# Low parts of the weights of the second layer's first FFN: VectorE subtraction or accumulating DMA

## The chip, the cores and the metric

The kernel runs on one core of one Trainium2 chip. What is measured is the device time of one execution in microseconds (us). One core has a TensorE (PE, matrix products; PEld is its weight load), a VectorE (DVE), a ScalarE (ACT), a GpSimd (POOL), a SyncE (SP) that issues the loads, and 16 DMA engines that all queues share.

## What is computed

Two small transformers stand one behind the other, on 256 positions of width 1024. The first has two layers, with modulation vectors made from a condition, and carries 256 context positions beside the 256 main ones, so that most of its products have 512 columns. Each layer is an FFN, a token mixer and a second FFN:

```
def _swiglu(h, w1, w3, w2):
    return (jax.nn.silu(h @ w1) * (h @ w3)) @ w2

for l in range(DEPTH):
    ml = _modulation(c, w_ada[l], b_ada[l])
    mc = _modulation(c_ctx[None], w_ada[l], b_ada[l])
    ffn1 = (ffn1_w1[l], ffn1_w3[l], ffn1_w2[l])
    lat = lat + 0.5 * ml[2] * _swiglu(_modulate(lat, norm_ffn1_g[l], ml[0], ml[1]), *ffn1)
    cx = cx + 0.5 * mc[2] * _swiglu(_modulate(cx, norm_ffn1_g[l], mc[0], mc[1]), *ffn1)
    ...
```

w1 and w3 are 1024 x 2816, w2 is 2816 x 1024, all float32. The second transformer (a retention and window layer, an axial attention layer, two MLPs) follows, and is not touched here.

## The kernel before, in words

The products with weights run on TensorE with operands in the type float32r. Each weight and each activation is held as a pair: hi, the value written as float32r, and lo, the value minus hi. mm3 makes three matmuls of each product: hi by hi (L294), hi weight by lo activation (L295), lo weight by hi activation (L296).

The weights lie in HBM in the order in which they are used, cut by plan() into 544 chunks of 128 x 1024 (w2's later thirds: 128 x 896). The class Weights brings them in. For each chunk, SP issues a load into one of 4 raw buffers (dma_to, L135), ACT copies raw into one of 6 hi buffers (hi_to, L145), and DVE writes raw minus hi into one of 5 lo buffers (lo_to, L156). A raw buffer is free again when DVE has read it, a hi or lo buffer when TensorE has done the last matmul on it.

Every engine works through its own queue in order, and the order is that in which the code emits the instructions. In the steady part (step) one chunk is one step: first its 24 matmuls, then the closing work of an earlier step (flush), then ahead_hi, then one tick of a background job, then ahead_lo. In the step of chunk b, ahead_hi goes up to chunk b+5 and ahead_lo up to b+4, as far as there are buffers; SP then loads up to 4 chunks beyond the last lo.

The second layer's first FFN is ffn(1, 0): 68 chunks, in three thirds of w1/w3 pairs (gated, L521 to L526: silu on ACT, product on DVE, hi copy on ACT, lo on DVE) followed by eight w2 chunks each. Its background job is ada: 32 tiles of 512 KB (L264) and a 1 MB condition tile (condb, L269; its silu on ACT is L272), and two DVE reductions a tile (L279), one tile a step.

The first four chunks are used before the steps begin, in tail, which closes the FFN before. I call these chunks F0 to F3, the next F4 and so on; w6 and w7 are the last two chunks of the FFN before. tail does the halves of w6 and w7 for the main positions, calls W.lo_to(W.n_take + 2), which prepares chunks up to F2, does the halves for the context positions, takes the row sums (stats, L369, L373) and broadcasts them (bcast, L383), and makes the new h (make_h: DVE L402, ACT L410, DVE L411). Then F0 to F2 run on the first half. F3 is taken only there, by a call of its own, and its pair is made at that point. Then the second half's h is made, F0 to F2 run on it, W.ahead() prepares F4 to F6, and F3's second half closes the turn.

Of the kernel before, what the change touches and what calls it, by code (L numbers as in the profile page):

```python
# [7 lines left out]
F32 = mybir.dt.float32  # L8
F32R = mybir.dt.float32r
U8 = mybir.dt.uint8  # L10
AF = mybir.ActivationFunctionType
ALU = mybir.AluOpType
# [14 lines left out]
def plan():  # L27

    out = []

    def ffn(l, nm):
        for t0, n in THIRDS:
            for j in range(t0, t0 + n):
                out.append((nm + "_w1", l, 0, 8, j * 128, 128))
                out.append((nm + "_w3", l, 0, 8, j * 128, 128))
            for o in range(8):
                out.append((nm + "_w2", l, t0 * 128, n, o * 128, 128))

    U, V, Q, FW, BW, I, OG = (i * 512 for i in range(7))
    for l in range(2):  # L40
        ffn(l, "ffn1")

        def cols(c0, n):
            for j in range(n):
                out.append(("w_in", l, 0, 8, c0 + j * 128, 128))

        def pairs(name, ly, c0, n):
            for j in range(n):
                out.append((name, ly, 0, 4, c0 + j * 256, 256))
                out.append((name, ly, 512, 4, c0 + j * 256, 256))  # L50

        cols(FW, 2), cols(BW, 2), cols(Q, 2)
        pairs("w_in", l, I, 2)
        cols(FW + 256, 2), cols(BW + 256, 2), cols(Q + 256, 2)
        pairs("w_in", l, V, 2)
        cols(OG + 256, 2), cols(OG, 2), cols(U, 4)
        for o in range(8):
            out.append(("w_out", l, 0, 8, o * 128, 128))
        ffn(l, "ffn2")

    def pairs2(name, c0, n):
        for j in range(n):
            out.append((name, 0, 0, 4, c0 + j * 256, 256))
            out.append((name, 0, 512, 4, c0 + j * 256, 256))

    def mlp(l):
        for j in range(32):
            out.append(("w_mlp_up_2", l, 0, 8, j * 128, 128))
        for o in range(8):
            for q in range(4):  # L70
                out.append(("w_mlp_down_2", l, q * 1024, 8, o * 128, 128))

    for c0, n in ((2048, 4), (4096, 1), (4352, 1), (3072, 4), (0, 2), (512, 2), (1024, 4)):
        pairs2("w_in_even_2", c0, n)
    for r0 in (1024, 0):
        for o in range(8):
            out.append(("w_out_even_2", 0, r0, 8, o * 128, 128))
    mlp(0)
    for c0, n in ((1024, 1), (0, 2), (1280, 1), (512, 2)):
        pairs2("w_in_odd_2", c0, n)  # L80
    for r0 in (0, 512):
        for o in range(4):
            out.append(("w_out_odd_2", 0, r0, 4, o * 256, 256))
    mlp(1)
    return out
# [22 lines left out]
class Pair:  # L108


    def __init__(self, hi, lo=None):
        self.t = [hi, lo]
# [5 lines left out]
class Weights:  # L118


    def __init__(self, nc, flat, rawp, hlp, sizes, nraw, nhl):
        self.nc, self.flat, self.rawp, self.hlp = nc, flat, rawp, hlp
        self.sizes, self.nraw, self.nhl = sizes, nraw, nhl
        self.offs = np.concatenate([[0], np.cumsum(np.array(sizes) * 128)]).tolist()
        self.n = len(sizes)
        self.n_dma = self.n_hi = self.n_lo = self.n_take = 0
        self.raw, self.hl = {}, {}
# [11 lines left out]
    def hi_to(self, i):  # L139
        while self.n_hi <= min(i, self.n - 1):  # L140
            j = self.n_hi
            self.dma_to(j)
            c = self.sizes[j]
            t = self.hlp.tile([128, 1024], F32R, tag="hi", name="hi", bufs=self.nhl)
            self.nc.scalar.activation(out=t[:, :c], in_=self.raw[j][:, :c], func=AF.Copy)  # L145
            self.hl[j] = Pair(t)
            self.n_hi += 1

    def lo_to(self, i):
        while self.n_lo <= min(i, self.n - 1):  # L150
            j = self.n_lo
            self.hi_to(j)
            c = self.sizes[j]
            t = self.hlp.tile([128, 1024], F32R, tag="lo", name="lo", bufs=self.nhl - 1)
            w = self.hl[j]
            self.nc.vector.tensor_tensor(  # L156
                out=t[:, :c], in0=self.raw.pop(j)[:, :c], in1=w[:, 0, :c].bitcast(F32), op=ALU.subtract)
            w.t[1] = t
            self.n_lo += 1
        self.dma_to(self.n_lo - 1 + self.nraw)  # L160
# [10 lines left out]
        self.ahead_lo(rate)  # L171

    def ahead_hi(self, rate=3):
        self.hi_to(min(self.n_hi + rate - 1, self.base + self.nhl - 1))

    def ahead_lo(self, rate=3):
        self.lo_to(min(self.n_lo + rate - 1, self.base + self.nhl - 2))
# [2 lines left out]
def build(tc, T):  # L180
    nc = tc.nc
    vo, nvec = vec_plan()
    sizes = [p[3] * p[5] for p in plan()]
    PS = bass.MemoryType.PSUM
    with ExitStack() as ctx, tc.manual_schedule():
        pool = lambda name, bufs, **k: ctx.enter_context(tc.tile_pool(name=name, bufs=bufs, **k))
# [2 lines left out]
        rawp = pool("rawp", 4)  # L189
        hlp = pool("hlp", 1)  # L190
# [3 lines left out]
        b1 = ctx.enter_context(ExitStack())  # L194
        hp = b1.enter_context(tc.tile_pool(name="hp", bufs=1))

        W = Weights(nc, T["wflat"], rawp, hlp, sizes, 4, 6)

        def tmp(n=512, dt=F32):
            return tp.tile([128, n], dt, tag="t", name="t")  # L200
# [1 line left out]
        def mm_ps():  # L202
            return psm.tile([128, 512], F32, tag="mm", name="mm")
# [94 lines left out]
        def mmA(ps, w, X, nk, t0, t1, k0=0, k1=None, first=True):  # L298

            k1 = nk if k1 is None else k1  # L300
            for k in range(k0, k1):
                mm3(ps[:, t0:t1], w[:, 0, k * 128:(k + 1) * 128], w[:, 1, k * 128:(k + 1) * 128],
                    X[k][:, 0, t0:t1], X[k][:, 1, t0:t1], k == 0, k == nk - 1)
# [3 lines left out]
        def flush():  # L307
            while epis:
                epis.pop(0)()
# [4 lines left out]
        def step(fn, epi=None, rate=3, parts=1):  # L314

            for i, f in enumerate(fn if isinstance(fn, list) else [fn]):
                f()
                if i == 0:
                    flush()
                    W.ahead_hi(rate)  # L320
                    if not lo_last[0]:
                        W.ahead_lo(rate)
                pace[0] += 1
# [3 lines left out]
                if i == 0 and lo_last[0]:  # L327
                    W.ahead_lo(rate)
            if epi is not None:
# [94 lines left out]
        def group_start():  # L424
            ws = W.take(4)
            return ws, [mm_ps() for _ in range(4)]
# [6 lines left out]
        def norm_group(l, i, halves, more=()):  # L433
# [4 lines left out]
            for half, dg in zip(halves, dgs):  # L438
# [3 lines left out]
                for c in range(4):  # L442
                    mmA(ps[c], ws[c], h, 8, half[0], half[1], 4, 8)
                    W.base = W.n_take - 4 + c
                    W.ahead(1)
            return ps
# [538 lines left out]
        with ExitStack() as ph:  # L985
# [106 lines left out]
            for i in range(2):  # L1092
                t = tmp()
# [156 lines left out]
        class Attn:  # L1250


            def __init__(self, kT, vv, bias, sink, perm, scale, pool):
                self.kT, self.vv, self.bias, self.sink, self.perm, self.scale, self.pool = (
                    kT, vv, bias, sink, perm, scale, pool)
                self.heads, self.done = [], 0
# [164 lines left out]
        with ExitStack() as ph:  # L1421
# [99 lines left out]
            for j in range(4):  # L1521
                proj(lambda p, b, j=j: nc.scalar.activation(
                    out=sg[:, b, j * 256:(j + 1) * 256], in_=p[:, :256], func=AF.Silu, scale=rr[:, b:b + 1]),
# [99 lines left out]
            for o in range(8):  # L1623
                (w,) = W.take(1)
                p = mm_ps()
# [6 lines left out]
            for o in range(8):  # L1632
                (w,) = W.take(1)
                p = mm_ps()
# [35 lines left out]
        with ExitStack() as ph:  # L1670
# [34 lines left out]
            for j in range(4):  # L1705
                proj(lambda p, b, j=j: epi_q(p, b, j))
                if j == 1:
                    proj(lambda p, b: nc.scalar.activation(
                        out=vb[:, b, :], in_=p[:, :256], func=AF.Copy, scale=rr[:, b:b + 1]))
# [34 lines left out]
            for half in range(2):  # L1744
# [14 lines left out]
                for o2 in range(2, 4):  # L1759
                    (w,) = W.take(1)  # L1760
                    for i in range(2):
                        o = 2 * o2 + i
                        p = mm_ps()
# [132 lines left out]
```

## Time and profile before

| | us |
|---|---|
| median of 3 runs | 2420.7 (2420.54 to 2421.33) |
| the profiled execution | 2421.72 |
| its span, first to last instruction | 2419.9 |
| PE busy | 2392.5 (99%) |
| DVE busy | 1565.7 (65%) |
| ACT busy | 1013.0 (42%) |
| POOL busy | 58.5 (2%) |
| DMA engines, mean busy share | 45% |

The rows below name a line of the kernel (L156 is line 156), the engine, and output <- inputs. Busy times of different engines lie beside each other. A view by windows shows what each engine did in a stretch; a view of waits shows who had to stand still and for whom; a timeline shows single instructions with their start and length. PE's lengths overlap, since matmuls are pipelined: the distance of two starts is what one costs.

### The profile page before, as it was taken

To read this page: it belongs to the slowest core of one execution; us is meant where nothing else is said; L and a number is where in the kernel's file an instruction comes from. 1 tells how busy PE (TensorE), PEld (TensorE's weight loads), DVE (VectorE), ACT (ScalarE), POOL (GpSimd) and SP (SyncE) were. 2 spreads that over 40 slices of the span, in tenths; PEclk is the share of its full clock that TensorE was granted. 3 is DMA by queue.
4 is the path that set the end of the run, shared out by engine and by line. 5 is a ranking of instruction groups with operands and counts; after the bars stand their busy time and mean duration, and the time that the engine had idled before them with its cause. 6 is when DMAs were issued, how large, how long until landed. Compare 5 with 4: busy or idle time off the path is not lost.

```text
span 2419.9 us, 37688 instructions
## 1 busy us (share of the span) xinstructions
PE 2392.5 (99%) x15240; PEld 2145.0 (89%) x15240; DVE 1565.7 (65%) x2498; ACT 1013.0 (42%) x1649; POOL 58.5 (2%) x102
## 2 busy tenths in 40 slices
PE   7999999999999999999999999999999999999999
PEld 5888888999888888898888899999999999999999
DVE  6777876736478784468763366765576676557753
ACT  4322223455342222342222353654467556446642
POOL 0000000000000000000000000000002000010000
PEclk9999999999999999999999999999999999999999
DMA  8555552312245453235543232345655365553653
GB/s 311 201 191 175 200 190 70 104 54 70 79 160 198 178 196 112 89 133 198 184 149 102 87 100 84 114 157 187 186 193 169 127 201 185 192 166 114 209 190 125
DMA packets 107791, 370.88 MB, mean 153 GB/s; under 512 B 11864, under 2 KB 18008, under 8 KB 107232
## 3 DMA queue, kind: packets, MB, share of 16 engines
q1 hardware_dynamic: 107616, 368.47, 44.9%
q8 instruction: 120, 1.97, 0.3%
q14 instruction: 55, 0.45, 0.1%
HBM read 367.36 MB, written 1.06 MB: 152 GB/s over the span
## 4 chain that ended last, share of the span: by engine, by line
PE 91%; DVE 3%; issue 3%; ACT 2%; DMA 0%; POOL 0%; POOLq 0%; SPq 0%; DVEq 0%; ACTq 0%
PE mm L295 26%; PE mm L296 26%; PE mm L294 26%; PE mm L655 2%; PE mm L1188 2%; PE mm L1189 2%; PE mm L1187 2%; DVE lo L156 1%; PE mm L850 1%; PE mm L849 1%; PE mm L851 1%; ACT hi L145 0%; PE aux L383 0%; PE mm L1284 0%; PE aux L369 0%
## 5 line engine op out<-in xcount | busy, mean ns | idle before, releaser
L294 PE MATMUL mm<-h,hi 128*128 128x512 f32 (+1 forms) x2460 | 834.6, 339 | 3.0 <-ACT h L410 1.9
L296 PE MATMUL mm<-h,lo 128*128 128x512 f32 (+1 forms) x2460 | 829.8, 337 | 0.4 <-DVE lo L156 0.2
L145 ACT ACTIVATE hi<-raw 128x1024 fp32r<-128x1024 f32 (+1 forms) x544 | 563.5, 1042 | 527.1 <-PE mm L295 312.5
L156 DVE TENSOR_TENSOR lo<-raw,hi 128x1024 fp32r<-128x1024 f32 (+1 forms) x544 | 652.3, 1205 | 141.1 <-issue 55.8
L295 PE MATMUL mm<-l,hi 128*128 128x512 f32 (+1 forms) x2076 | 722.6, 348 | 1.1 <-DVE l L1074 0.2
L294 PEld LDWEIGHTS mm<-h,hi 128*128 128x128 f32 x2460 | 465.0, 189 | 56.7 <-ACT h L410 2.2
L296 PEld LDWEIGHTS mm<-h,lo 128*128 128x128 f32 x2460 | 464.7, 189 | 55.0 <-DVE lo L156 1.2
L295 PEld LDWEIGHTS mm<-l,hi 128*128 128x128 f32 x2076 | 392.5, 189 | 56.1 <-DVE l L411 2.7
L294 PE MATMUL mm<-g,hi 128*128 128x256 f32 (+1 forms) x1258 | 409.3, 325 | 0.0
L295 PE MATMUL mm<-g,hi 128*128 128x256 f32 (+1 forms) x1258 | 408.8, 325 | 0.0
L296 PE MATMUL mm<-g,lo 128*128 128x256 f32 (+1 forms) x1258 | 408.8, 325 | 0.0
L279 DVE CUSTOM_DVE_ANT_0 jk<-ada,condb,vec 128x1024 f32<-128x1024 f32 x256 | 328.1, 1282 | 11.7 <-ACT condb L272 7.2
L295 PEld LDWEIGHTS mm<-g,hi 128*128 128x128 f32 x1258 | 236.8, 188 | 22.2
L294 PEld LDWEIGHTS mm<-g,hi 128*128 128x128 f32 x1258 | 236.9, 188 | 22.1
L296 PEld LDWEIGHTS mm<-g,lo 128*128 128x128 f32 x1258 | 236.8, 188 | 22.0
L525 ACT ACTIVATE g<-t 128x512 fp32r<-128x512 f32 (+1 forms) x88 | 50.9, 578 | 350.8 <-DVE t L523 350.8
L417 DVE SCALAR_TENSOR_TENSOR xT<-mm,mods,xT 128x256 f32<-128x256 f32 x192 | 86.0, 479 | 135.7 <-PE mm L296 135.5
L523 DVE TENSOR_TENSOR t<-t,mm 128x512 f32<-128x512 f32 (+1 forms) x88 | 54.6, 620 | 181.2 <-PE mm L296 179.1
L295 PE MATMUL mm<-h,hi 128*128 128x256 f32 x512 | 143.9, 281 | 0.0
L1187 PE MATMUL mm<-hi,h 128*128 128x256 f32 x384 | 111.2, 289 | 0.0
L1188 PE MATMUL mm<-lo,h 128*128 128x256 f32 x384 | 107.6, 280 | 0.1
L1189 PE MATMUL mm<-hi,h 128*128 128x256 f32 x384 | 107.4, 280 | 0.0
(295 smaller groups left out, 2406.7 us busy)
## 6 DMA issues: line engine op xcount, KB each, us to landing
raw<-wflat SPq DMA_DIRECT2D x480, 512.0 KB, 3.4
ada<-adaT SPq DMA_DIRECT2D x128, 512.0 KB, 4.3
raw<-wflat SPq DMA_DIRECT2D x64, 448.0 KB, 3.3
ada<-ada SPq DMA_DIRECT2D x16, 512.0 KB, 10.0
condb<-condb SPq DMA_DIRECT2D x3, 1024.0 KB, 9.5
xT<-xT SPq DMA_DIRECT2D x2, 1024.0 KB, 5.7
bias<-d SPq DMA_DIRECT2D x2, 1024.0 KB, 7.5
out<-t SPq DMA_DIRECT2D x8, 128.0 KB, 1.9
```

What stands on the lines that cost most here:

```text
L145: self.nc.scalar.activation(out=t[:, :c], in_=self.raw[j][:, :c], func=AF.Copy)
L156: self.nc.vector.tensor_tensor(out=t[:, :c], in0=self.raw.pop(j)[:, :c], in1=w[:, 0, :c].bitcast(F32), op=ALU.subtract)
L279: nc.vector.tensor_tensor_reduce(out=jk, in0=t, in1=condb[:, c, :], scale=1.0, scalar=V(f"bada{l}")[:, j:j + 1], op0=ALU.mult, op1=ALU.add ...
L294: nc.tensor.matmul(out, whi, xhi, start=start, stop=False)
L295: nc.tensor.matmul(out, whi, xlo, start=False, stop=False)
L296: nc.tensor.matmul(out, wlo, xhi, start=False, stop=stop)
L417: nc.vector.scalar_tensor_tensor(out=xT[:, o, t0:t1], in0=ps[:, t0:t1], scalar=gate(l, i, o, 0 if t0 == 0 else 1), in1=xT[:, o, t0:t1], op ...
L523: nc.vector.tensor_tensor(out=m[:, :t1], in0=s[:, :t1], in1=pb[:, :t1], op=ALU.mult)
L525: nc.scalar.activation(out=t[:, 0, :t1], in_=m[:, :t1], func=AF.Copy)
L1187: nc.tensor.matmul(p[:, :256], xhi, whi, start=(k == 0), stop=False)
L1188: nc.tensor.matmul(p[:, :256], xhi, wlo, start=False, stop=False)
L1189: nc.tensor.matmul(p[:, :256], xlo, whi, start=False, stop=(k == 7))
```

## The change

For the 68 chunks of the second layer's first FFN (by_dma), VectorE no longer makes lo. ACT writes the hi copy as before, and directly behind it a second copy, minus hi, into the lo buffer. Then GpSimd issues a DMA that adds raw onto that buffer, so that raw minus hi stands in it. This DMA reads raw and lo in SBUF and writes lo. Both are emitted in hi_to, and lo_to passes over these chunks. Since lo is now written where hi is, ahead_hi goes one chunk less far for them (b+4 in the step of chunk b). The raw buffer is free again when the DMA has landed. In the changed file the lines below L118 stand 1 to 12 lines later; L150 is the negated copy, L151 the DMA.

```diff
--- before.py
+++ after.py
@@ -118,7 +118,8 @@
 class Weights:
 
 
-    def __init__(self, nc, flat, rawp, hlp, sizes, nraw, nhl):
+    def __init__(self, nc, flat, rawp, hlp, sizes, nraw, nhl, by_dma=()):
+        self.by_dma = by_dma
         self.nc, self.flat, self.rawp, self.hlp = nc, flat, rawp, hlp
         self.sizes, self.nraw, self.nhl = sizes, nraw, nhl
         self.offs = np.concatenate([[0], np.cumsum(np.array(sizes) * 128)]).tolist()
@@ -144,6 +145,12 @@
             t = self.hlp.tile([128, 1024], F32R, tag="hi", name="hi", bufs=self.nhl)
             self.nc.scalar.activation(out=t[:, :c], in_=self.raw[j][:, :c], func=AF.Copy)
             self.hl[j] = Pair(t)
+            if j in self.by_dma:
+                lo = self.hlp.tile([128, 1024], F32R, tag="lo", name="lo", bufs=self.nhl - 1)
+                self.nc.scalar.activation(out=lo[:, :c], in_=t[:, :c].bitcast(F32), func=AF.Copy, scale=-1.0)
+                self.nc.gpsimd.dma_start(
+                    out=lo[:, :c].bitcast(F32), in_=self.raw.pop(j)[:, :c], accum_op=ALU.add)
+                self.hl[j].t[1] = lo
             self.n_hi += 1
 
     def lo_to(self, i):
@@ -151,6 +158,9 @@
             j = self.n_lo
             self.hi_to(j)
             c = self.sizes[j]
+            if j in self.by_dma:
+                self.n_lo += 1
+                continue
             t = self.hlp.tile([128, 1024], F32R, tag="lo", name="lo", bufs=self.nhl - 1)
             w = self.hl[j]
             self.nc.vector.tensor_tensor(
@@ -171,7 +181,7 @@
         self.ahead_lo(rate)
 
     def ahead_hi(self, rate=3):
-        self.hi_to(min(self.n_hi + rate - 1, self.base + self.nhl - 1))
+        self.hi_to(min(self.n_hi + rate - 1, self.base + self.nhl - 1 - (self.n_hi in self.by_dma)))
 
     def ahead_lo(self, rate=3):
         self.lo_to(min(self.n_lo + rate - 1, self.base + self.nhl - 2))
@@ -180,7 +190,9 @@
 def build(tc, T):
     nc = tc.nc
     vo, nvec = vec_plan()
-    sizes = [p[3] * p[5] for p in plan()]
+    chunks = plan()
+    sizes = [p[3] * p[5] for p in chunks]
+    by_dma = {j for j, p in enumerate(chunks) if p[1] == 1 and p[0].startswith("ffn1")}
     PS = bass.MemoryType.PSUM
     with ExitStack() as ctx, tc.manual_schedule():
         pool = lambda name, bufs, **k: ctx.enter_context(tc.tile_pool(name=name, bufs=bufs, **k))
@@ -194,7 +206,7 @@
         b1 = ctx.enter_context(ExitStack())
         hp = b1.enter_context(tc.tile_pool(name="hp", bufs=1))
 
-        W = Weights(nc, T["wflat"], rawp, hlp, sizes, 4, 6)
+        W = Weights(nc, T["wflat"], rawp, hlp, sizes, 4, 6, by_dma)
 
         def tmp(n=512, dt=F32):
             return tp.tile([128, n], dt, tag="t", name="t")
```

**On ACT, at the turn to this FFN.** The numbers tell buffers apart; F0, F1 and F2 are the three 128x1024 hi copies. Before:

```order
L145 ACTIVATE hi_8053<-raw_7961 128x1024 [waits DMAHW0_49,PE_49]
L357 ACTIVATE t_8084<-xT_88 128x512 [waits DVE_49,Activation_49]
L145 ACTIVATE hi_8086<-raw_7992 128x1024 [waits DMAHW1_49,PE_49,Activation_49]
L357 ACTIVATE t_8117<-xT_88 128x512 [waits DVE_49,Activation_49]
L145 ACTIVATE hi_8119<-raw_8024 128x1024 [waits DMAHW2_49,PE_49]
L357 ACTIVATE t_8128<-xT_88 128x512 [waits DVE_49,Activation_49]
L456 ACTIVATE t_8177<-xT_88 128x256 [waits DVE_49,Activation_49]
L456 ACTIVATE t_8179<-xT_88 128x256 [waits DVE_49,Activation_49]
L373 ACTIVATE r_8211<-aux_8208,epsc_85 128x2 [waits PE_49]
```

Now:

```order
L146 ACTIVATE hi_8084<-raw_7961 128x1024 [waits DMAHW0_49,PE_49]
L150 ACTIVATE lo_8086<-hi_8084 128x1024 [waits PE_49,Activation_49]
L369 ACTIVATE t_8116<-xT_88 128x512 [waits DVE_49]
L146 ACTIVATE hi_8118<-raw_7992 128x1024 [waits DMAHW1_49]
L150 ACTIVATE lo_8120<-hi_8118 128x1024 [waits PE_49,Activation_49]
L369 ACTIVATE t_8128<-xT_88 128x512 [waits DVE_49]
L468 ACTIVATE t_8177<-xT_88 128x256 [waits DVE_49]
L468 ACTIVATE t_8179<-xT_88 128x256 [waits DVE_49]
L146 ACTIVATE hi_8183<-raw_8024 128x1024 [waits DMAHW2_49]
L150 ACTIVATE lo_8185<-hi_8183 128x1024 [waits PE_49,Activation_49]
L385 ACTIVATE r_8214<-aux_8211,epsc_85 128x2 [waits PE_49]
```

F0 and F1 are made one square later than before, each with its negated copy. F2's pair has moved behind both 128x256 squares, to just ahead of the row-sum instruction (r).

**On ACT, where F3 is made.** The first row is the row-sum instruction of the second half, h0 to h2 belong to that half's make_h. Before:

```order
L373 ACTIVATE r_8355<-aux_8352,epsc_85 128x2 [waits PE_49,Pool_49]
L145 ACTIVATE hi_8376<-raw_8057 128x1024 [waits DMAHW3_49]
L410 ACTIVATE h0_8242<-t_8409,mods1_95 128x256 [waits DVE_49]
L410 ACTIVATE h1_8244<-t_8411,mods1_95 128x256 [waits DVE_49]
L410 ACTIVATE h2_8246<-t_8415,mods1_95 128x256 [waits DVE_49]
```

Now:

```order
L385 ACTIVATE r_8358<-aux_8355,epsc_85 128x2 [waits PE_49,Pool_49]
L146 ACTIVATE hi_8379<-raw_8055 128x1024 [waits DMAHW3_49]
L150 ACTIVATE lo_8381<-hi_8379 128x1024 [waits Activation_49]
L422 ACTIVATE h0_8245<-t_8413,mods1_95 128x256 [waits DVE_49]
L422 ACTIVATE h1_8247<-t_8415,mods1_95 128x256 [waits DVE_49]
```

The negated copy has come in behind F3's hi. The DMA that completes it is the fourth of 68 that stand in one row on POOL, with nothing of POOL's own work between them.

**On SP, around the start of the background job.** raw are loads of weight chunks, ada the first of the background job's loads. Before:

```order
L135 DMA raw_8185<-wflat 128x1024 [waits DMAHW2_49,DVE_49,Activation_49]
L135 DMA raw_8380<-wflat 128x1024 [waits DMAHW3_49,DVE_49]
L135 DMA raw_8525<-wflat 128x1024 [waits DMAHW4_49,DVE_49]
L135 DMA raw_8527<-wflat 128x1024 [waits DMAHW5_49,DVE_49]
L135 DMA raw_8529<-wflat 128x1024 [waits DMAHW6_49,DVE_49]
L264 DMA ada_8608<-adaT 128x1024
```

Now:

```order
L136 DMA raw_8188<-wflat 128x1024 [waits DMAHW2_49,DMASW2_49,Activation_49]
L136 DMA raw_8384<-wflat 128x1024 [waits DMAHW3_49,DMASW3_49,Activation_49]
L136 DMA raw_8532<-wflat 128x1024 [waits DMAHW4_49,DMASW4_49,Activation_49]
L136 DMA raw_8534<-wflat 128x1024 [waits DMAHW5_49,DMASW5_49,Activation_49]
L136 DMA raw_8536<-wflat 128x1024 [waits DMAHW6_49,DMASW6_49,Activation_49]
L276 DMA ada_8619<-adaT 128x1024
```

The order is the same, but each load of a raw buffer waits for an accumulating DMA (DMASW) where it waited for DVE, and the loads of the background job stand behind those.

## Rows read from the trace of the kernel before

**Rows 1.** Page: busy time and share of each engine; shares of the chain that ended last.

```profile
PE 2392.5 (99%) x15240; PEld 2145.0 (89%) x15240; DVE 1565.7 (65%) x2498; ACT 1013.0 (42%) x1649; POOL 58.5 (2%) x102
...
PE 91%; DVE 3%; issue 3%; ACT 2%; DMA 0%; POOL 0%; POOLq 0%; SPq 0%; DVEq 0%; ACTq 0%
```

**Rows 2.** Windows of the changed stage; the first row names the columns.

```profile
core 0: us, PE busy (x) PEld busy (x) DVE busy (x) ACT busy (x) POOL busy (x), PEclk, DMA share, GB/s
...
1030.00:1060.00 30.00, 29.62 (x242) 28.71 (x241) 20.82 (x47) 11.45 (x25) 0.00 (x0) 1.00 0.15 51
1060.00:1140.00 80.00, 80.00 (x373) 65.82 (x372) 58.68 (x79) 30.55 (x38) 0.00 (x0) 1.00 0.56 204
1140.00:1250.00 110.00, 110.00 (x473) 88.70 (x472) 85.68 (x127) 26.24 (x32) 0.00 (x0) 1.00 0.53 183
1250.00:1440.00 190.00, 189.68 (x956) 159.20 (x955) 85.93 (x140) 57.59 (x81) 0.00 (x0) 1.00 0.28 91
```

**Rows 3.** Waits of PE, 1000 to 1480 us: total us, times, longest.

```profile
PE mm L655 <- DVE Y L637: 0.5, 1, 0.5
PE mm L296 <- DVE lo L156: 0.2, 1, 0.2
```

**Rows 4.** Page: the hi copies and the subtractions; count, busy us, mean ns.

```profile
L145 ACT ACTIVATE hi<-raw 128x1024 fp32r<-128x1024 f32 (+1 forms) x544 | 563.5, 1042 | 527.1 <-PE mm L295 312.5
L156 DVE TENSOR_TENSOR lo<-raw,hi 128x1024 fp32r<-128x1024 f32 (+1 forms) x544 | 652.3, 1205 | 141.1 <-issue 55.8
```

**Rows 5.** Timeline of ACT at the turn: start us, length us, instruction.

```profile
1027.08 0.63 ACT L357 ACTIVATE t<-xT 128x512 f32<-128x512 f32 x1 [3.32 <-DVE xT L417]
...
1036.55 0.42 ACT L456 ACTIVATE t<-xT 128x256 f32<-128x256 f32 x1 [2.06 <-DVE xT L417]
1038.81 0.26 ACT L373 ACTIVATE r<-aux,epsc 128x2 f32<-128x2 f32 x1 [1.84 <-PE aux L369]
...
1059.56 0.51 ACT L410 ACTIVATE h<-t,mods 128x256 fp32r<-128x256 f32 x1 [0.28 <-DVE t L402]
1059.97 1.99 ACT L145 ACTIVATE hi<-raw 128x1024 fp32r<-128x1024 f32 x2
```

**Rows 6.** Timeline of PE at the turn.

```profile
1043.04 0.28 PE L295 MATMUL mm<-l,hi 128*128 128x256 f32 x1
1043.16 0.28 PE L296 MATMUL mm<-h,lo 128*128 128x256 f32 x1
...
1067.07 0.40 PE L296 MATMUL mm<-h,lo 128*128 128x512 f32 x1
```

**Rows 7.** Chain that ended last, the pieces around F3: start us, length us.

```profile
1049.46 0.96 ACT hi L145
1050.44 1.24 DVE lo L156
1051.73 0.39 PE mm L296
```

**Rows 8.** DMA issues: count, KB each, median us from issue to landing.

```profile
raw<-wflat SPq DMA_DIRECT2D x480, 512.0 KB, 3.4
...
condb<-condb SPq DMA_DIRECT2D x3, 1024.0 KB, 9.5
xT<-xT SPq DMA_DIRECT2D x2, 1024.0 KB, 5.7
```

**Rows 9.** Windows of the stage after the next mixer, around a pause of PE.

```profile
1592.40:1594.90 2.50, 1.50 (x13) 1.42 (x12) 0.82 (x2) 0.42 (x1) 0.00 (x0) 1.00 0.01 3
1594.90:1598.00 3.10, 1.22 (x5) 0.93 (x4) 2.67 (x4) 1.21 (x2) 0.00 (x0) 0.50 0.10 24
1598.00:1605.10 7.10, 6.36 (x28) 6.13 (x29) 6.27 (x17) 4.98 (x10) 0.00 (x0) 0.50 0.40 137
```

**Rows 10.** Timeline of PE in that stretch.

```profile
1600.06 0.41 PE L295 MATMUL mm<-l,hi 128*128 128x256 f32 x1
1600.28 0.41 PE L296 MATMUL mm<-h,lo 128*128 128x256 f32 x1
```

## The prediction

> **What bounds the kernel now.** I began with the shares of the page [rows 1]. TensorE is busy 99% of the span and is 91% of the chain that ended last; VectorE, which the change relieves, is 3% of that chain. Then I read the changed stage by windows, to see whether VectorE is the limit there and only there [rows 2]. It is not: from 1060 to 1440 us PE is busy in 379.7 of 380 us, also in the stretch where DVE is fullest (85.7 of 110 us). In 110 us PE starts 473 matmuls, so a chunk of 24 lasts 5.6 us. Last I read whom PE waits for in this stage [rows 3]: 0.7 us in all, 0.2 of it for a low part, once. So what the change can give back here is at most that, and with the idle time in the windows (0.4 us from 1030 to 1060, 0.3 from 1250 to 1440) about 1 us. The question is what the new path of a low part costs where PE needs it soon.
>
> **The change part by part.**
>
> Removed: 68 subtractions of about 1.2 us on DVE [rows 4], some 80 us of an engine that PE does not wait for. Worth: the one wait of 0.2 us, counted below.
>
> Added on ACT: 68 negated copies. They have the shape of the hi copies, so 1.04 us each [rows 4], 71 us in all. In the steps, ACT is busy 26 of 110 us and would be so for 47 [rows 2]; a gated pair's silu and copy can come late by a step or more before PE lacks a buffer. Cost nothing there. At the turn two of them matter, below.
>
> Added on POOL and the DMA engines: 68 accumulating DMAs of 512 KB. No row shows one. I call T the time from the end of the negated copy until TensorE may read the low part. From below, T is bounded by a load of 512 KB, 3.4 us from issue to landing; from above by the slowest 1 MB load, condb behind three others, 9.5 us [rows 8]. An accumulate reads two tiles of 512 KB, so the nearest row is the plain 1 MB load of xT, 5.7 us; I take T = 5.7. The DMA engines' time for one is separate from T: two loads a chunk take 0.53 of 5.6 us, 1.5 us each [rows 2], so two reads take 3.0 us.
>
> The Trainium skill (Collectives: The Full Stack, the bandwidth ceiling) says that an add in the DMA path costs nothing itself, but that its second read goes through the same ring and halves the rate; no run here shows it, and it speaks for the 3.0 us. Another page (DMA: Bandwidth & Descriptors, anatomy of one DMA) fits 2.0 us plus bytes over 436 GB/s for a DMA that GpSimd issues: an estimate by it with 1 MB read is 4.4 us, and the sum of waits below would then be 4.4 us instead of 7.5.
>
> Is the lead long enough? In the steps, yes: the negated copy of chunk b+4 ends about 3.5 us into the step of b (an estimate: a gated copy, the hi copy and itself are 2.7 us [rows 4], the rest waiting for the product), and PE needs the chunk 4 x 5.6 = 22.4 us after that step began. That leaves 22.4 - 3.5 - 5.7 = 13 us. F1's copies, behind the square that starts at 1027.08 [rows 5], end at about 1029.7, and its DMA lands near 1035.4, 7 us before PE needs it; F0 is one step of 5 us earlier, which also covers a slow first DMA. At the turn it is short three times, because F2, F3 and F4 are made just in time there:
>
> F2: hi and its negated copy come behind the second 128x256 square, which starts at 1036.55 and lasts 0.42 [rows 5]. Two copies of about 1.0 us back to back (two take 1.99 us in the same rows) end at 1038.95; the DMA lands at 1044.65. PE first reads F2's low part at 1043.16 [rows 6]. Wait 1.5 us. The row-sum instruction behind them starts at 1038.81 today, so they delay it by 0.1 us, and DVE's subtraction of F2, which stood before the reciprocal, is gone for about as much: zero.
>
> F3: the chain that ended last shows it whole [rows 7]: hi at 1049.46 for 0.96, DVE's subtraction at 1050.44, PE at 1051.73. Now the negated copy ends at about 1051.45 and the DMA lands at 1057.15, where PE started at 1051.73. Wait 5.4 us, the old wait being in it. Nothing hides this: PE's queue is in order, and everything behind F3's third matmul, the broadcast for the second half and the new h too, moves by the same amount.
>
> F4: the hi copies start at 1059.97 [rows 5]; hi and negated copy end at 1061.95, the DMA lands at 1067.65, PE needs it at 1067.07 [rows 6]. Wait 0.6 us. F5 and F6 have 3 us or more beyond this.
>
> Sum of waits: 1.5 + 5.4 + 0.6 = 7.5 us. With T = 3.4 it is 0 + 3.1 + 0 = 3.1; with T = 9.5 it is 5.3 + 9.2 + 4.4 = 18.9.
>
> What the pause at F3 does to TensorE's clock: the trace has one pause of PE of that size. From 1592.4 it has only small matmuls (x13 in 2.5 us), and at 1594.9 the granted clock falls from 1.00 to 0.50 (2.4 to 1.2 GHz) and stays so until 1605.1 [rows 9]. At the low level two matmuls of 256 columns start 0.22 us apart, else 0.12 [rows 6, 10]. If the pause at F3 (from 1051.4 on, 5.7 us with the old wait) does the same, the clock falls 2.5 us into it and is low for 10.2 us, of which PE still waits 3 and works 7.2. That work takes 7.2 x (1 - 0.12/0.22) = 3.3 us longer.
>
> The Trainium skill (TensorE: Matmul & The Clock Gate, part 1) calls 1.2 GHz the default state, which activity releases and idleness brings back; the rows at 1594.9 agree (0.50 behind a pause). By that rule the sum is 10.8 us, without it 7.5.
>
> Moved: SP's loads of raw tiles now wait for the DMA, and the background job's first loads stand behind three such waits. The loads of F8 to F10 wait for the DMAs of F4 to F6, which brings ada and condb later by about T and two copies, 5.7 + 2.1 = 8 us (an estimate). ACT stands at condb's silu for at most that long, and what is queued behind it are copies for chunks with 13 us of lead: covered; if the cover were gone it would cost those 8 us. In the 32 steps with an ada load the DMA engines would have 3.0 + 2 x 1.5 = 6.0 us of work in 5.6 us: 0.4 x 32 = 13 us of backlog, just the cover; afterwards it is 4.5 us and drains. The price is zero, with little to spare.
>
> **The rivals.**
>
> Waits without the clock: the pause is cut in two or falls otherwise, and PE's clock holds. 7.5 us. For it: the pause of the rows lasted until after 1598, longer than the one at F3, and one case is no rule.
>
> A short DMA: T is 4.5 us or less. F2 and F4 then wait 0.3 us at most and F3 4.2 us, 4.5 us in all and the clock may hold: within 0.2% (4.8 us; about what a measurement of this kernel tells from no change). At T = 3.4 it is 3.1 us. For it: the transfer stays in SBUF and the stretch has little traffic (DMA share 0.15 [rows 2]). Against: two reads, and a queue that the kernel has not used so far.
>
> The DMA engines do not keep up: this turns a fixed cost into one for each chunk. It decides from 2.6 us of all engines per accumulate while ada is loaded (5.6 - 3.0) with 13 us of cover, and from 4.1 us afterwards. If the two reads and the write add up to three passes, 4.5 us, the ada steps lack 1.9 us each, 32 x 1.9 - 13 = 48 us, the other 30 lack 0.4, 12 us, and the turn costs about 15 with T = 7.2: +75 us, 2496 us. Against: reads and writes of a plain load run side by side.
>
> The other side, faster: the freed VectorE shortens PE's path. It decides only if T is below the subtraction's own 1.2 us, since F3's low part must come earlier than today; no DMA row is near that (3.4 at least). The price is the 1 us of idle time, 2419.7 us, still within 0.2%.
>
> **How the numbers follow.** The profiled execution is 2421.7 us, 1.8 beyond its span and 1.0 above the median. Waits and clock add 10.8: 2432.5 in a profiled execution, 2431.5 against the median of 2420.7. Chances: forecast (waits and clock, T about 5 to 8) 0.42; waits alone 0.19 (2428.2); longer T, to 9.5, with the clock 0.08 (2420.7 + 18.9 + 3.3 = 2443); short DMA 0.15 (2424 to 2425); DMA engines behind 0.14 (2440 to 2500); faster 0.02. The range goes from 2423.5 (T = 3.4 without the clock) to 2452, so that it holds all but most of the DMA-bound case and a little below. Faster by over 0.2%: 0.02. Within 0.2%: 0.15. Slower: 0.83.
>
> **What would show it.** In the changed kernel's profile: PE's longest wait at F3, on the accumulating DMA, 5 to 6 us; one of 1 to 2 us at F2 and under 1 us at F4; then none to the end of the stage, with 5.6 us a chunk. A granted clock of 0.50 for about 10 us behind F3. DVE's busy time down by some 80 us, ACT's up by 71. If PE waits in the steps between 1100 and 1250 with the DMA share near 1, the third rival is right. If the wait at F3 is under 4 us, T is short. If PE shows no wait at F3, my reading of the order is wrong.

## The result, and the profile after

| | before | after |
|---|---|---|
| median of 3 runs, us | 2420.7 (2420.54 to 2421.33) | 2437.27 (2435.29 to 2438.58) |
| ratio to before | | 1.0067 (95% interval 1.0044 to 1.009) |
| the profiled execution / its span, us | 2421.72 / 2419.9 | 2437.27 / 2435.4 |

The change makes the kernel 16.6 us slower; the forecast was 10.8. The page of after, shares and chain, against [rows 1]; below them the DMA queues, of which q0 holds the accumulating DMAs (packets, MB, share of 16 engines):

```profile
PE 2396.8 (98%) x15240; PEld 2147.0 (88%) x15240; DVE 1491.0 (61%) x2430; ACT 1080.2 (44%) x1717; POOL 120.7 (5%) x170
...
q1 hardware_dynamic: 107616, 368.47, 44.1%
q0 software_dynamic: 9792, 34.61, 7.6%
...
PE 85%; issue 6%; DVE 4%; DMA 3%; ACT 2%; POOL 0%; POOLq 0%; SPq 0%; DVEq 0%; ACTq 0%
```

DVE works 74.7 us less, ACT 67.2 more, and DMA is now 3% of the chain. 7.6% of 2435.4 us, over 68, is 2.7 us of all DMA engines for one accumulate.

The windows of the stage, against [rows 2]:

```profile
core 0: us, PE busy (x) PEld busy (x) DVE busy (x) ACT busy (x) POOL busy (x), PEclk, DMA share, GB/s
1030.00:1060.00 30.00, 24.75 (x189) 23.97 (x188) 12.42 (x30) 10.50 (x19) 2.45 (x3) 0.92 0.51 123
1060.00:1140.00 80.00, 80.00 (x394) 67.05 (x394) 35.71 (x61) 43.12 (x52) 12.16 (x14) 0.99 0.86 237
1140.00:1250.00 110.00, 103.97 (x435) 82.91 (x434) 65.10 (x108) 47.30 (x52) 17.44 (x20) 0.97 1.01 288
1250.00:1440.00 190.00, 189.87 (x895) 156.44 (x894) 53.43 (x100) 82.60 (x105) 26.19 (x30) 1.00 0.73 179
```

PE is idle in two places, 5.3 us at the turn and 6.0 us after 1140, and hardly at all elsewhere in these windows. From 1140 to 1250 the DMA share has nearly doubled, from 0.53 to 1.01. Whom PE waited for, against [rows 3] (1000 to 1490 us; total, times, longest):

```profile
PE mm L306 <- ACT g L537: 6.0, 1, 6.0
PE mm L308 <- DMA lo<-raw: 5.1, 2, 4.7
PE mm L667 <- DVE Y L649: 0.5, 1, 0.5
```

Both traces hold the same 15240 matmuls in the same order, so the start of each can be compared with that of its twin. After lags by -0.2 us before the turn, 7.1 behind it (place 1062 of before), still 7.1 at 1128, 16.1 at 1145, 16.2 at 1590 and 15.4 at the end. So there are two losses, **7.2 us at the turn** and **9.0 us at one place between 1128 and 1145**, and no cost for a chunk as such.

**The turn.** ACT, POOL and PE of after around F3, against [rows 5 to 7]:

```profile
1049.88 1.05 ACT L146 ACTIVATE hi<-raw 128x1024 fp32r<-128x1024 f32 x1
1050.96 1.06 ACT L150 ACTIVATE lo<-hi 128x1024 fp32r<-128x1024 f32 x1
```

```profile
1052.31 0.86 POOL L151 DMA_DIRECT2D lo<-raw  x1 [12.35 <-ACT lo L150]
```

```profile
1051.81 0.28 PE L307 MATMUL mm<-l,hi 128*128 128x256 f32 x1
1056.75 0.58 PE L308 MATMUL mm<-h,lo 128*128 128x256 f32 x1 [4.66 <-DMA lo<-raw]
1057.13 0.42 PE L306 MATMUL mm<-h,hi 128*128 128x256 f32 x1
1057.35 0.41 PE L307 MATMUL mm<-l,hi 128*128 128x256 f32 x1
```

The negated copy ends at 1052.02, PE reads the low part at 1056.75: T is 4.7 us. Then matmuls start 0.22 us apart, as in [rows 10]. The windows around both pauses show why (the second pair is the second loss):

```profile
1055.24:1056.75 1.51, 0.00 (x0) 0.00 (x0) 0.00 (x0) 0.00 (x0) 0.00 (x0) 0.50 0.67 130
1056.75:1062.07 5.32, 5.32 (x25) 5.32 (x26) 1.74 (x5) 0.91 (x2) 0.00 (x0) 0.50 0.30 99
...
1150.81:1151.98 1.17, 0.00 (x1) 0.00 (x1) 0.47 (x2) 0.68 (x2) 0.00 (x0) 0.50 1.05 298
1151.98:1157.64 5.66, 5.66 (x13) 4.20 (x14) 2.32 (x4) 4.40 (x5) 1.74 (x2) 0.50 1.02 305
```

The granted clock is 0.50 (1.2 GHz) from 1055.24 to 1062.07, and PE works in 5.32 us of it: 5.32 x (1 - 0.12/0.22) = 2.4 us lost.

**The second loss** is at the first w2 chunk of the first third. SP, DVE, ACT and PE of after there:

```profile
1133.29 0.38 SPq L276 DMA_DIRECT2D ada<-adaT  x1
1141.27 0.33 SPq L136 DMA_DIRECT2D raw<-wflat  x1
1141.69 0.48 SPq L276 DMA_DIRECT2D ada<-adaT  x1
```

```profile
1148.04 1.28 DVE L291 CUSTOM_DVE_ANT_0 jk<-ada,condb,vec 128x1024 f32<-128x1024 f32 x1 [4.43 <-DMA ada<-adaT]
1149.25 0.08 DVE L291 DVE_READ_ACCUMULATOR2_ANT mods<- 128x1 f32 x1
1149.37 1.28 DVE L291 CUSTOM_DVE_ANT_0 jk<-ada,condb,vec 128x1024 f32<-128x1024 f32 x1
1150.58 0.08 DVE L291 DVE_READ_ACCUMULATOR2_ANT mods<- 128x1 f32 x1
1150.58 0.68 DVE L535 TENSOR_TENSOR t<-t,mm 128x512 f32<-128x512 f32 x1
```

```profile
1151.30 0.63 ACT L537 ACTIVATE g<-t 128x512 fp32r<-128x512 f32 x1 [6.38 <-DVE t L535]
```

```profile
1145.56 0.40 PE L308 MATMUL mm<-g,lo 128*128 128x512 f32 x1
1151.98 0.80 PE L306 MATMUL mm<-g,hi 128*128 128x512 f32 x1 [6.03 <-ACT g L537]
```

Read it from the bottom. PE lacks g, the last gated pair of the third. Its copy on ACT waits for DVE's product, and that stands in DVE's queue behind an ada tile which arrives at 1148. This tile was requested at 1141.69, right behind a raw load for which SP had stood since 1133.7, because the raw buffer's accumulating DMA had not landed. The kernel before at the same place, ACT and PE:

```profile
1134.79 0.63 ACT L525 ACTIVATE g<-t 128x512 fp32r<-128x512 f32 x1 [5.03 <-DVE t L523]
```

```profile
1133.80 0.40 PE L294 MATMUL mm<-g,hi 128*128 128x512 f32 x1
...
1138.70 0.40 PE L294 MATMUL mm<-g,hi 128*128 128x512 f32 x1
```

The first w2 chunk takes the eight g of the third, three matmuls each; the last is needed by its 22nd matmul, at 1138.70. Before, that g was ready at 1135.42: **3.3 us of slack**, where a pair inside a third, whose g is read only at the third's end, has steps. The wait is 6.0 us, and the low clock behind it costs 13 matmuls 0.435 instead of 0.233 us, 2.6 us.

How long DMAs take to land, 1100 to 1260 us (count, KB, median us), before and after:

```profile
ada<-adaT SPq DMA_DIRECT2D x25, 512.0 KB, 4.4
raw<-wflat SPq DMA_DIRECT2D x20, 512.0 KB, 3.4
```

```profile
ada<-adaT SPq DMA_DIRECT2D x29, 512.0 KB, 6.5
lo<-raw POOLq DMA_DIRECT2D x27, 512.0 KB, 7.2
raw<-wflat SPq DMA_DIRECT2D x25, 512.0 KB, 6.1
```

### The profile page after: what moved, and what is told of

The parts are those of the page before. It is cut to its first block, busy times and chain, and to the rows that moved or that the text cites. A ratio compares the mean times of both kernels' runs of the same rounds, so it can differ in the third digit from the quotient of the medians.

```text
span 2435.4 us, 37810 instructions
## 1 busy us (share of the span) xinstructions
PE 2396.8 (98%) x15240; PEld 2147.0 (88%) x15240; DVE 1491.0 (61%) x2430; ACT 1080.2 (44%) x1717; POOL 120.7 (5%) x170
## 3 DMA queue, kind: packets, MB, share of 16 engines
HBM read 367.36 MB, written 1.06 MB: 151 GB/s over the span
## 4 chain that ended last, share of the span: by engine, by line
PE 85%; issue 6%; DVE 4%; DMA 3%; ACT 2%; POOL 0%; POOLq 0%; SPq 0%; DVEq 0%; ACTq 0%
PE mm L307 24%; PE mm L308 24%; PE mm L306 24%; PE mm L667 2%; PE mm L1200 1%; PE mm L1201 1%; PE mm L1199 1%; DMA raw<-wflat 1%; DVE lo L166 1%; PE mm L861 1%; PE mm L863 1%; PE mm L862 1%; DMA lo<-raw 1%; DMA ada<-adaT 1%; ACT hi L146 1%
## 5 line engine op out<-in xcount | busy, mean ns | idle before, releaser
L166 DVE TENSOR_TENSOR lo<-raw,hi 128x1024 fp32r<-128x1024 f32 (+1 forms) x476 | 571.8, 1207 | 121.1 <-PE mm L308 52.9
```

The costliest lines, as they stand in the source:

```text
L166: self.nc.vector.tensor_tensor(out=t[:, :c], in0=self.raw.pop(j)[:, :c], in1=w[:, 0, :c].bitcast(F32), op=ALU.subtract)
```

## The experiments

Two theories of the second loss stood against each other: **order** (ada's loads stand on SP behind raw loads that wait for an accumulate) and **load** (the DMA engines are full while ada is loaded). All kernels are edits of the changed one. Differences are against runs of the kernel before that were measured beside them: 2420.26 us (first four), 2420.65 (second four), 2420.95 (last four).

| kernel | median us | more than before, us | ratio, 95% interval |
|---|---|---|---|
| f3_only | 2427.79 | 7.5 | 1.0018 to 1.0043 |
| no_turn | 2430.52 | 10.3 | 1.0028 to 1.0058 |
| ada_one | 2427.84 | 7.6 | 1.0019 to 1.0042 |
| raw3 | 2430.35 | 10.1 | 1.0027 to 1.0057 |
| no_turn_raw3 | 2425.63 | 5.0 | 1.0012 to 1.0029 |
| late_only | 2421.09 | 0.4 | 0.9992 to 1.001 |
| hold | 2431.64 | 11.0 | 1.0032 to 1.0057 |
| copy | 2424.94 | 4.3 | 1.0008 to 1.0026 |
| ada_act | 2430.36 | 9.4 | 1.0025 to 1.005 |
| no_turn_ada_act | 2422.56 | 1.6 | 0.9998 to 1.0016 |
| half_ada | 2428.45 | 7.5 | 1.0018 to 1.004 |
| every_other | 2421.55 | 0.6 | 0.9993 to 1.001 |

**f3_only**: only F3 goes by DMA.

```
+    by_dma = {min(by_dma) + 3}
```

> Only chunk F3 gets its low part from the accumulating DMA, all others from VectorE as before. Theory: a fixed cost of the turn, no cost per chunk. TensorE waits 4.6 us at F3 (copy's end to TensorE 4.7 us, as in the changed kernel), the granted clock falls to 0.50 behind that pause for some 7 us, of which 5.3 us are work: 2.4 us more. No other wait in the stage. 2420.7 + 7 = 2427.7. Rival (the clock fell for the sum of the pauses or for another cause): no fall, 2425.3. Rival (most of the loss comes from the many DMAs, the turn is harmless): within 2 us of 2420.7.

Measured 7.5 us. The one wait is 4.9 us at F3, the clock is 0.50 for 6.8 us from 1054.3, and the lag grows by 6.8 us there and nowhere else in the stage. One pair made just in time carries the whole cost of the turn.

**no_turn**: F0 to F3 by VectorE, the other 64 by DMA.

```
+    by_dma -= {min(by_dma) + i for i in range(4)}
```

> F0 to F3 by VectorE as before, the other 64 chunks by DMA. The turn then costs nothing (F4 had no wait in the changed kernel). Theory: the second loss, 9.0 us at the end of the first third of w1/w3 (wait for the gated pair, and a second fall of the clock), is independent of the turn and stays: 2429 to 2430. Rival (the second loss is an echo of the first, since the late turn also made the background job's loads late): it goes too, 2421.

Measured 10.3 us: the turn is clean, but PE waits 2.0 us for low parts and, at the third's end, 4.6 for a gated pair, with the clock low behind it. The second loss does not come from the turn.

**ada_one**: 31 of the stage's 32 ada loads are left out.

```
-            todo, tiles = list(range(t0, t1)), []
+            todo, tiles = list(range(t0, t1) if t0 != 40 else [t0]), []
...
-                t = tiles.pop(0)
+                t = tiles.pop(0) if t0 != 40 else tiles[0]
```

> All 68 chunks by DMA; of the 32 tiles of the background job in this stage only the first is loaded, and all its reductions read that one (31 loads of 512 KB left out, so the modulation values are not the reference's). Theory: VectorE's wait for these tiles holds the last gated pair before w2, so the 9.0 us go and the turn's 7.2 stay: 2428. Rival (the pair is held by ScalarE, which has 71 us more work, or by POOL): the wait of 6 us stays, 2437.

Measured 7.6 us, the turn and half a microsecond for a low part. The second loss needs the ada loads. Whether by their bytes or their place on SP, this run can't say: it takes both away.

**raw3**: SP fetches raw tiles three chunks ahead, so that a raw load waits for an older accumulate.

```
-        self.dma_to(self.n_lo - 1 + self.nraw)
+        self.dma_to(self.n_lo - 1 + self.nraw - (self.n_lo - 1 in self.by_dma))
```

> All 68 chunks by DMA, but SyncE loads raw tiles only 3 chunks ahead instead of 4, so that a load's buffer has been released one step earlier and SyncE does not stand there; same bytes, same engines. Theory S (queue order: the background job's loads stand on SyncE behind raw loads that wait up to 8 us for an accumulating DMA): the second loss goes, the turn stays, 2428. Theory B (the DMA engines, at a share of 0.98 to 1.05, cannot move it in time): the wait at the end of the first third stays within 2 us of 6, 2435 to 2438.

Measured 10.1 us: the gated wait falls from 6.0 to 0.2, for order. But 2.6 us beyond the turn stay, and the next kernel shows that it isn't the whole answer.

**no_turn_raw3**: both edits.

> F0 to F3 are made by VectorE again, the other 64 chunks by the accumulating DMA, and SP brings raw tiles three chunks ahead for those. If the whole loss consists of the two pieces named so far, the fixed one at the turn (7 us) and SP's raw loads that hold up the loads of ada (9 us), then both are gone here and what is left are the small waits that showed beside them, 0.6 to 1.5 us: 2421 to 2422.5 us, no wait of a gated pair over 0.5 us and a PE delay below 2 us to the end of the stage. If the DMA engines themselves are short (they are about 0.99 busy while ada is loaded), a loss that grows with the chunks remains: 2424 us or more.

Measured 5.0 us (2423.02 to 2428.46 over 11 runs): too much for order alone. Its waits of PE and its stage:

```profile
PE mm L307 <- ACT g L538: 3.1, 1, 3.1
```

```profile
1100.00:1140.00 40.00, 37.84 (x163) 30.12 (x161) 25.68 (x41) 20.99 (x24) 6.95 (x8) 1.00 1.05 303
```

```profile
lo<-raw POOLq DMA_DIRECT2D x12, 512.0 KB, 8.6
raw<-wflat SPq DMA_DIRECT2D x11, 512.0 KB, 9.4
ada<-adaT SPq DMA_DIRECT2D x11, 512.0 KB, 10.7
```

The gated wait is back although the order is eased. The DMA share is 1.05, and an ada tile (last fence, 1090 to 1150 us) lands 10.7 us after its issue. That the transfers lack the 7 us which the pause at the turn gave them is my reading and not shown: in raw3, with that pause, ada takes 10.0 us to land in the same stretch.

**late_only**: DMA only from F40 on, behind the last ada load.

```
+    by_dma -= {min(by_dma) + i for i in range(40)}
```

> The accumulating DMA only from F40 on, that is, behind the last load of ada; F0 to F39 are made by VectorE as before. 28 of 68 chunks then still go the new way. If the new path costs nothing for each chunk as such, and only where a pair is made just in time or where loads of ada stand behind raw loads, this is the kernel before: 2420.3 us within 1 us, no new wait of PE. If each accumulate costs something (contention in SBUF, more queue work), 28 of 68 parts of what is neither turn nor ada remain: 1 us or more, and it is seen as a steady growth of PE's delay from F40 to the end of the stage. The freed VectorE can give at most the few tenths that PE waits there today.

Measured 0.4 us, with no new wait of PE. 28 chunks go the new way for nothing, and the freed VectorE gives nothing either.

**hold**: no ada tile in the two steps of a third's last pair.

```
+                        pace[:] = [0, 99] if (l, i) == (1, 0) and j == j0 + nj - 1 else [0, 1]
```

> The changed kernel, but in the two steps of the last gated pair of each third the background job rests (no ada tile is taken there). Theory: at a third's end VectorE stands at an ada tile that is late, the last pair's product stands behind it in VectorE's queue, and the first w2 chunk needs that pair at once. Then the wait of 6 us and the clock low behind it go, and the turn alone remains: 2428 us (2427 to 2430). Rival: the pair is late because ScalarE stands at a raw tile, or because the low part of a w2 chunk is late; then the wait stays and the time is 2436 to 2438. In between (2431 to 2434): the tile of the step before is late enough to hold VectorE too.

Measured 11.0 us, 5.6 less than after, where 9 was expected. DVE of this kernel at the third's end:

```profile
1141.85 0.69 DVE L538 TENSOR_TENSOR g<-t,g 128x512 fp32r<-128x512 f32 x1 [0.70 <-ACT g L537]
1146.41 0.69 DVE L535 TENSOR_TENSOR t<-t,mm 128x512 f32<-128x512 f32 x1 [3.87 <-ACT t L533]
```

No ada tile is in front of the last pair any more, and PE's wait falls from 6.0 to 1.4, with no fall of the clock behind it. What remains is late on ACT's silu, and 1.1 us are low parts before 1128. VectorE standing at an ada tile is most of the wait, not all.

**copy**: the DMA copies raw instead of adding, so it reads one tile and not two.

```
-                    out=lo[:, :c].bitcast(F32), in_=self.raw.pop(j)[:, :c], accum_op=ALU.add)
+                    out=lo[:, :c].bitcast(F32), in_=self.raw.pop(j)[:, :c])
```

> The DMA on GpSimd's queue copies raw over the negated copy instead of adding onto it: one tile of 512 KB is read instead of two, everything else is as in the changed kernel (lo then holds raw and not raw minus hi, so the third matmuls of this stage multiply other numbers). If the second read is what makes the accumulate longer than a load, the time from the copy's end to TensorE at F3 falls from 4.7 to about 3.4 us (a plain load of 512 KB) and the wait there from 4.7 to 3.3; the DMA engines' time per chunk falls from 2.7 to about 1.4 us, SP stands less, and the wait of 6 us at the third's end goes or shrinks: 2425 to 2429 us. It also tells whether a pause of 3.6 us is still followed by a granted clock of 0.50 (if not, 2424). If the length is a fixed cost of a DMA that GpSimd issues, F3 waits 4.7 us as in the changed kernel and the turn costs 7 us; 2427 us or more.

Measured 4.3 us. Its DMA queue, and PE at F3:

```profile
q0 software_dynamic: 8768, 34.61, 3.6%
```

```profile
1054.16 0.39 PE L308 MATMUL mm<-h,lo 128*128 128x256 f32 x1 [3.08 <-DMA lo<-raw]
```

One read takes 3.6% x 2423.0 / 68 = 1.3 us of the engines instead of 2.7; T is 3.2 us instead of 4.7 (its negated copy ends at 1051.00). The clock still falls, for 3.4 us. The second loss is gone, with SP's order as in after: that speaks for load.

**ada_act**: ada is loaded from ACT's queue, at the same bytes.

```
-                    nc.sync.dma_start(out=t, in_=T["adaT"][l, todo.pop(0)])
+                    (nc.sync if t0 != 40 else nc.scalar).dma_start(out=t, in_=T["adaT"][l, todo.pop(0)])
```

> The changed kernel, but the loads of ada are issued from ScalarE's queue and no longer from SP's, so they don't stand behind raw loads that wait for an accumulating DMA; bytes and DMAs are the same. If the order on SP is the cause of the second loss, the tiles come in time, the wait of the last gated pair (6.0 us) and the clock low behind it go, and the turn alone remains: 2427 to 2429 us. If the DMA engines are full while ada is loaded (0.99 busy, a load takes 6.8 us to land and not 4.4), it does not matter from which queue the loads come: 2433 to 2438 us, with waits of the gated pair or of low parts at the end of the first third. New risk: ScalarE waits for a free ada buffer and holds its own copies; then the time is above 2438.

Measured 9.4 us, the turn and 1.9 more. PE's waits, and its stage:

```profile
PE mm L308 <- DMA lo<-raw: 5.1, 2, 4.7
PE mm L667 <- DVE Y L649: 0.5, 1, 0.5
PE mm L306 <- ACT g L537: 0.4, 1, 0.4
```

```profile
1100.00:1140.00 40.00, 40.00 (x173) 32.22 (x172) 24.71 (x40) 21.47 (x24) 6.98 (x8) 1.00 1.05 309
```

The engines are as full as ever (1.05), yet the gated wait is 0.4. That speaks for order.

**no_turn_ada_act**: the same without the turn.

> The same with F0 to F3 made by VectorE, so that no pause at the turn gives the transfers time to catch up. Order on SP as the cause: 2420.5 to 2422 us, no wait. Full DMA engines as the cause: as in the kernel with F0 to F3 by VectorE alone, 2428 to 2432 us, or at least 2425 us as in the one that also loads raw three ahead (3.1 us of wait at the third's end).

Measured 1.6 us, against 10.3 with ada on SP. One wait for a low part of 1.3 us, near 1090, is left, no gated one.

**half_ada**: ada's loads bring half a tile, at the same order. VectorE multiplies this half twice, so that its time stays (that part of the edit is left out here).

```
-                    nc.sync.dma_start(out=t, in_=T["adaT"][l, todo.pop(0)])
+                    q = 1024 if t0 != 40 else 512
+                    nc.sync.dma_start(out=t[:, :q], in_=T["adaT"][l, todo.pop(0)][:, :q])
...
```

> The changed kernel, but each ada tile of this stage brings only its first 512 columns (VectorE multiplies these twice, so its time and all queues keep their order); half of each dot product of the modulation vectors is thus another one. A step with ada then asks the DMA engines for 2.7 + 1.4 + 0.7 = 4.8 us instead of 5.5 us of 5.6. If full DMA engines are the cause, the second loss of 9 us goes at unchanged queue order: 2427 to 2429 us, DMA share below 0.95 there. If the order on SP alone is the cause, the tiles still come late by a whole step and most of the wait stays: 2433 us or more.

Measured 7.5 us, the turn and 0.3 us for a low part. PE waits for no gated pair, though SP's queue has the order of after. The DMA share is still 1.03 from 1100 to 1140, above what I expected and above after's 0.98, and 0.92 from 1160 to 1250 (after: 1.01). So the share alone does not tell whether time is lost; the landings differ more (ada 5.9 us, after 8.2, from 1090 to 1150).

**every_other**: every second chunk by DMA, from F5 on.

```
+    by_dma = {j for j in by_dma if j - min(by_dma) > 3 and (j - min(by_dma)) % 2}
```

> F0 to F3 by VectorE, and from F5 on only every other chunk by the accumulating DMA: 32 of 68, spread over the whole stage, those of the steps with ada too. A step with ada asks the DMA engines for 2.7 / 2 + 2 x 1.4 = 4.1 us on average of 5.6 us. If full engines are the cause, nothing is lost: 2420 to 2421.5 us, no new wait of PE. If a single accumulate in front of an ada load is enough (order), waits of a gated pair of 1 us or more show up: 2423 us or more.

Measured 0.6 us, interval around 1, no new wait; from 1100 to 1140 the DMA share is 0.89 where after has 0.98. So neither theory is enough by itself. Full engines make each landing late (medians of 6 to 11 us, where before had 3.4 and 4.4); SP's order turns a late accumulate into an ada load that is issued late; the short slack at the third's end turns that into a wait. Easing the bytes (copy, half_ada, ada_one) removes all of the second loss; easing the order removes some 80% of it in ada_act and about half in no_turn_raw3 (10.3 to 5.0). A queue of its own does not make ada's transfers quicker: in ada_act a tile takes 9.1 us to land (after: 8.2), but the one in front of the last pair is issued at 1132.61 and not at 1141.69.

One cause was not separated from the order, the late start of the job. ACT's silu of condb, behind which the reductions begin, in after and in ada_act:

```profile
1100.57 1.91 ACT L284 ACTIVATE condb<-condb 128x2048 f32<-128x2048 f32 x1 [11.78 <-DMA condb<-condb]
```

```profile
1093.63 1.92 ACT L284 ACTIVATE condb<-condb 128x2048 f32<-128x2048 f32 x1 [3.19 <-DMA condb<-condb]
```

The last ada tile and the last pair's product on DVE in before:

```profile
1129.86 1.28 DVE L279 CUSTOM_DVE_ANT_0 jk<-ada,condb,vec 128x1024 f32<-128x1024 f32 x1
...
1134.07 0.69 DVE L523 TENSOR_TENSOR t<-t,mm 128x512 f32<-128x512 f32 x1 [1.78 <-PE mm L296]
```

The reductions end at 1131.1 and the product starts 2.9 us later; with the 3.3 us of slack this tile, the tenth, can be 6.2 us late for nothing. The table says how late the first reduction and that on the tenth tile start, against before and less what PE itself is late just ahead of the third's end:

| kernel | first tile, us | tenth tile, us | PE's wait for a gated pair, us |
|---|---|---|---|
| after | 13.2 | 12.5 | 6.0 |
| no_turn | 14.4 | 12.3 | 4.6 |
| no_turn_raw3 | 13.2 | 9.5 | 3.1 |
| raw3 | 11.6 | 6.5 | 0.2 |
| ada_act | 6.2 | 5.8 | 0.4 |
| no_turn_ada_act | 8.3 | 4.3 | 0 |
| half_ada | 6.8 | 2.8 | 0 |
| every_other | 8.2 | 1.1 | 0 |
| copy | 6.3 | 0.0 | 0 |

The wait follows the tenth tile's lateness beyond 6.2 us. But ada_act also starts the job 7.0 us less late, probably since condb no longer stands behind three ada tiles on SP (it lands in 11.7 us instead of 18.1), and the 6.7 us that it gains at the tenth tile are no more than that. raw3 starts nearly as late as after and catches up 5.1 us where after catches up 0.7. So the order on SP counts for the later tiles too (raw3); how much the late start, their order and the full engines bring was not tried one by one.

No version beats the kernel before: the best of them equal it, as the stage had under 1 us of waiting to give.

## Why the prediction was right, and where not

- **VectorE's relief is worth nothing**: right. DVE lost 74.7 us (80 forecast), PE's waits did not fall. late_only shows it clean.
- **ACT's copies**: 67 us more (71 forecast), 1.06 us each; by themselves they cost nothing in the steps, as late_only (28 of them) and copy (all of them, nothing lost behind the turn) show.
- **T**: 5.7 forecast, 4.7 measured at F2 and F3 (bounds 3.4 to 9.5). I took the 1 MB load of xT as nearest; two tiles in SBUF land sooner than that: the three accumulates between 1030 and 1056 have a median of 4.4 us from issue to landing. The estimate by the Trainium skill's fit (DMA: Bandwidth & Descriptors, anatomy of one DMA), 4.4 us for 1 MB read, was nearer; by the prediction's own rows its sum of waits is 4.3 us, not the 4.4 given there.
- **Waits at the turn**: F2 0.45 (1.5), F3 4.7 (5.4), F4 none (0.6); sum 5.1 instead of 7.5, nearly all from the shorter T.
- **Clock behind F3**: it fell as said, but 3.2 us into the pause instead of 2.5, and for 6.8 us, where the row of before had 10.2; 2.4 us instead of 3.3. Turn in all 7.2 us instead of 10.8.
- **DMA engines' time**: 3.0 forecast, 2.7 measured, 1.3 for one read. The Trainium skill (Collectives: The Full Stack, the bandwidth ceiling) says of a ReduceScatter that the add's second read halves the rate. Copy against after agrees for this DMA (1.3 to 2.7).
- **The step that failed is "Moved", priced at zero.** It saw the late ada and condb loads and a backlog of 13 us, and set them against 13 us of lead. Condb's load was issued 7.9 us late (1082.48 against 1067.49, less the 7.1 of the turn; 8 forecast), but then took 18.1 us to land where it took 9.5, a term that the step left out, and ACT began on it 13.2 us late. But this lead belongs to low parts. Who stands at a late ada tile is DVE, and behind it in its queue are the gated pairs. Of these the prediction said that they "can come late by a step or more before PE lacks a buffer". That holds inside a third and not at its end, where g itself is read within 4.9 us, with 3.3 us of slack. It cost 9.0 us.
- **The third rival** (DMA engines behind) named the right resource and nearly the right threshold (2.6 us an accumulate while ada is loaded; measured 2.7, share 0.98 to 1.04). The sign that the prediction gave for it, PE waiting between 1100 and 1250 with the DMA share near 1, came. Its form was wrong: not a cost for each chunk, but one wait where the slack is shortest, after which, as I read it, the pause itself gives the transfers time. At the end of the second third (its first w2 chunk starts at 1273.09) DVE has done its last ada tile, at 1269.4, and nothing is lost.

So the forecast was 5.8 us short by two errors of opposite sign, 3.6 us too much at the turn and 9.0 too little behind it. The mechanism of the turn was foreseen; that the sum came as near as it did is in part luck, since more than half of the loss comes from a step priced at zero. The small rest lies outside the stage: the low clock at the next mixer lasts 6.8 us in after and 10.2 in before [rows 9], which gives back 1.3 (it changes from kernel to kernel, 10.2 in f3_only, 6.8 in late_only), and the profiled execution of before was 1.0 above its median.

## What to carry to other kernels

Before moving work from an idle engine to the DMA path, look for the few places where its result is made just in time: the cost sits there, once, and not in the steady part. Follow every transfer that stands behind a new wait on its queue to its reader, and that reader's queue to the point where PE uses the result; the cover to compare with is the shortest one on that way (here 3.3 us at a third's end, 6.2 from the ada tile on), not the lead of the moved operation. And add up the DMA engines' time per step, here with 2.7 us for an accumulate and some 1.4 for a load (an estimate from the share of 0.51 of before between 1100 and 1140): at 4.1 (every_other) and 4.8 (half_ada) of 5.6 us nothing was lost at the third's end, at 5.5 the landings of the loads went from 3.4 and 4.4 us to 6.1 and 6.5.

## What the runs showed of the hardware

- An accumulating DMA of 512 KB inside SBUF, issued by GpSimd: 4.4 us from issue to landing in a quiet stretch, 7 to 10 us at a DMA share near 1; 0.87 us of POOL; 2.7 us of all engines, against 1.3 us for the plain copy.
- In this stage, pauses of PE of 3.1 us (copy, no_turn_raw3) to 6.0 us were all followed by a granted clock of 0.50 (1.2 GHz); in copy it came only at 1054.4, just after PE had begun again at 1054.16, and lasted 3.4 us. The waits of 1.4 us and less had none behind them.
